# RWKV recurrence: the chunks of a head tile in turn, with norm, gate and output projection by pairs of head tiles inside the loop

## The chip, the cores and the metric

One NeuronCore of a Trainium2 chip runs the whole program. The metric is the time of one execution on the device, in microseconds (us). Engines are named as in the profile: PE is TensorE (matmuls; PEld its weight loads), DVE is VectorE, ACT is ScalarE, POOL is GpSimd, SP is SyncE, whose queue issues the transfers.

## The reference

A block of one hybrid layer (an RG-LRU beside attention, then a mixture of experts) is followed by four layers of FFN, mixer, FFN on 256 tokens of 1024 channels, batch 1, all in fp32. The mixers of layers 0 and 3 are RWKV-7 with 16 heads of 64; layer 1 is Mamba-2, layer 2 sliding-window attention. What the change touches is the end of the RWKV mixer:

```python
def step(state, inp):
    r_t, w_t, k_t, v_t, kk_t, a_t = inp
    sa = jnp.einsum('bhvk,bhk->bhv', state, -kk_t)
    state = (state * w_t[:, :, None, :] + sa[..., None] * (kk_t * a_t)[:, :, None, :]
             + v_t[..., None] * k_t[:, :, None, :])
    return state, jnp.einsum('bhvk,bhk->bhv', state, r_t)
...
mean = jnp.mean(y, axis=-1, keepdims=True)
var = jnp.mean(jnp.square(y - mean), axis=-1, keepdims=True)
y = ((y - mean) * lax.rsqrt(var + RW_GN_EPS)).reshape(bsz, seq, d) * ln_w + ln_b
bonus = jnp.sum(rh * kh * r_k, axis=-1, keepdims=True) * vh
out = ((y + bonus.reshape(bsz, seq, d)) * g).astype(h.dtype) @ w_o
...
x = x + gate[:, 1, None] * y
```

Layer 3 also mixes its values with those of layer 0 (`v_first`).

## The kernel before

Channels lie on the 128 partitions, in J = 8 tiles of 128 (two heads each); tokens lie along the free axis, T = 256 of them. The residual stream `x` is [128, 8, 256].

**Projections.** A weight slab is 1 MB, [128, 2048], loaded by SP into one of 4 buffers (tag `raw`). `slab` (lines 315 to 331) splits it in two halves of 1024 columns: ScalarE rounds a half to `hi`, VectorE takes `lo` = raw - hi; there are 3 buffers of each. `mm3` multiplies hi by the activations' hi and lo parts and lo by their hi part: three matmuls of 128x128 weights and 256 columns. `proj` runs slab after slab of 256 output channels over all eight tiles of input channels, and calls back with the sum in PSUM. `proj_parts` is the same with a stop after each quarter.

**PSUM.** Eight banks under three tags: `y` has four, `h` two, `m` two (`bank`, lines 306 to 308). The products of a step (`pk`, two banks) are in `y`; `pw`, `pa`, the turned keys, the gate's products `pg` and half of the joins are in `h`; `py`, `pS`, the broadcasts `hb` and the other joins are in `m`.

**The recurrence** (`rwkv`, lines 650 to 1080) goes by two chunks of 128 tokens. A step is one chunk c of one head tile m, and the 16 steps go through chunk 0 of all tiles and then chunk 1 of all:

```python
steps = [(c, m) for c in range(2) for m in range(J)]
```

A step has four parts, each on TensorE with a copy behind it: `products` (keys against receptances and rates, masked by VectorE, two steps ahead), `weighted` (pw, copied to ws, two steps ahead), `solve` (pa = inverse times ws, copied to sa, one step ahead) and `finish` (py, copied to Y; for chunk 0 also the state S0, which chunk 1 of the same tile reads). The inverses of I - M come from 32x32 blocks by `join(g)`, four stages for eight blocks of `Mab`; two joins of small matmuls serve chunk 0 (block index 16 c + 2 m + e) and two chunk 1. Stages of the joins and quarters of the values' projections are handed out step by step. From step 5 on, `gated` puts one tile of the gate's products through ScalarE into G. In chunk 1, v is multiplied by the bonus sums and `squares` adds up the squares of Y, four tiles to a bank.

After the loop, `normal(0)` and `normal(1)` do the group norm of four tiles each: a chain of ten small VectorE operations (`rsqrt`, lines 445 to 463), a broadcast `hb`, three VectorE operations (lines 1017 to 1019) and a split. Then the output projection runs, four slabs over all of `oh`, `ol`:

```python
normal(0, *o)
normal(1, *o)
gate, nxt = now.gate(), follow()
...
self.proj("rw", 16 * j + 12, 4, on_o, uh=o[0], ul=o[1])
```

Its callback adds gate times the sum to x (`residual`, line 515) and lets the next FFN take the tile: `Follow.tile` squares it and splits A x (lines 503, 218, 219).

**Order.** Instructions are written in program order, but a planner puts each engine's queue in order by when it reckons operands and buffers to be free, earlier text first. A queue is then served strictly in that order. Chunks of the modulation vectors (`pump`: four passes of line 422 on VectorE and two loads) are put in at steps 1, 3, 5 and 7.

Of the kernel before, what the change touches and what calls it, by code (L numbers as in the profile page):

```python
# [10 lines left out]
F32 = mybir.dt.float32  # L11
F32R = mybir.dt.float32r
# [41 lines left out]
def shape_consts():  # L54
    """Masks, selectors and the like: they depend on shapes alone."""
# [33 lines left out]
def col_list(g):  # L89
    """Vectors as columns: 128 channels on the partitions, one column per 128."""  # L90
# [39 lines left out]
# query heads whose key heads sit on the same partitions, two to a tile  # L130
# [3 lines left out]
def prepare(g):  # L134
    """The inputs as the program reads them: moved, joined and padded, nothing computed."""
    g = {k: np.asarray(v) for k, v in g.items()}
    a = {}
# [24 lines left out]
    for j in range(2):  # L162
        rw += [kxm(g["rw_w_rkv_2"][j, i]) for i in (1, 0, 2)] + [kxm(g["rw_w_o_2"][j])]
# [31 lines left out]
# ---------------------------------------------------------------- the program  # L195
class Follow:
    """What a layer's part reads of x, taken as each tile of x is done: the squares, and A x, split,
    with the shift in a column of its own. W (A x r + shift) = r W (A x) + W shift, so the products
    with A x run before r, the reciprocal norm of a token, is known."""
# [45 lines left out]
    def scaled(self, h, t):  # L245
        """t = r times the product; the product with the shift comes as a column"""
# [7 lines left out]
class Store:  # L254
    """What follows the last part: x goes out, its last two tiles on their own"""
# [10 lines left out]
class Program:  # L266
# [42 lines left out]
    # ---- weights  # L309
# [5 lines left out]
    def slab(self, name, i, n=2):  # L315
        """The slab split in two, by halves: w(o) gives the hi and lo of columns o to o + 128."""
# [34 lines left out]
    def split(self, m, t, uh=None, ul=None):  # L351
        """t [128, 256] -> uh[m] + ul[m]"""
# [4 lines left out]
    def proj(self, name, base, n, cb, kt=J, uh=None, ul=None, pump=0):  # L357
        """Slabs of columns against the split activations: cb(slab, psum [128, tiles, 256])."""
# [7 lines left out]
    def proj_parts(self, name, i, cb, kt=J, uh=None, ul=None, tag="h"):  # L366
        """One slab, and a stop after each quarter"""
# [12 lines left out]
    # ---- modulation vectors  # L380
# [6 lines left out]
    def gemv(self, name, chunk, lhs, bias, out):  # L387
        """out [128, 4] = the chunk's 512 columns of lhs @ W + bias"""
# [19 lines left out]
    def silu_rows(self, name, cb):  # L408
        """cb [128, 1024] = silu of the vector, on every partition"""
# [5 lines left out]
    def gemv_v(self, name, chunk, bias, out):  # L415
        """The same on the vector engine, from a slab of rows: [128 columns, 2, 1024]"""
# [9 lines left out]
    def pump(self, n, on_vector=False):  # L426
        """The next n chunks of those for that engine"""
# [27 lines left out]
        # with h = v (8 / 3 y) ** 2: y = y (h - 10 / 3) h + 5 y, then Newton's step  # L455
# [9 lines left out]
    def ordered(self):  # L465
        """The vector engine's work traced inside stays behind the last that was marked"""
# [5 lines left out]
    def sum_d(self, st, src, first, last):  # L472
        """st [128 t, 2] += sum of src [128, 256] over its partitions"""
# [3 lines left out]
    def bcast_t(self, r):  # L477
        """r [128 t, 2] -> [128, 256], the same on every partition"""
# [5 lines left out]
    def head_stat(self, st, m, src):  # L484
        """st [128 t, 2, n] gets the sums of src [128, 256] over 64 partitions each"""
# [3 lines left out]
    def head_bcast(self, r, m, tag="m"):  # L489
        """r [128 t, 2, n] -> [128, 256]: heads 2m and 2m + 1, 64 partitions each"""  # L490
# [22 lines left out]
    def residual(self, m, y, gate, follow=None):  # L513
        """x[m] += gate * y"""
# [5 lines left out]
    def mod2(self, i, s):  # L520
        """A and shift columns of layer i's part s"""
# [17 lines left out]
    def modulate(self, src, bc, A, sh, dst=None, follow=None):  # L539
        """src * A * bc + sh, split, or into dst's last 256 columns"""  # L540
# [13 lines left out]
    def centred(self, xc, between=None):  # L554
        """xc = x - mean over the channels; the reciprocal deviation, on every partition"""
# [16 lines left out]
    def token_major(self, w, h):  # L572
        """h [128 t, 2, 256] = the split activations times a slab of 256 columns"""
# [9 lines left out]
    # ---- FFN  # L583
# [65 lines left out]
    # ---- RWKV-7  # L649
    def rwkv(self, l, now, follow):  # L650
# [4 lines left out]
        with ExitStack() as ctx:  # L655
# [24 lines left out]
            # decay and in-context rate: h W + dx (mu W)  # L680
# [18 lines left out]
            # keys  # L699
# [44 lines left out]
            # decay from the middle of the first chunk to the middle of the second  # L744
# [10 lines left out]
            # receptance; the keys against the rates  # L755
# [13 lines left out]
            def against(m):  # L769
# [13 lines left out]
                for e in range(2):  # L783
                    for c in range(2):
                        o = 16 * c + 2 * (m - 1) + e
                        tt(Mab[:, o:o + 3:2, :], pb[e][:, c], self.k("mtri")[:, None, 0:P].to_broadcast([P, 2, P]),
# [1085 lines left out]
```

## Time and profile before

| | us |
|---|---|
| median of 3 runs | 3163.48 |
| lowest and highest | 3135.44, 3188.22 |
| span of the profiled execution | 3161.7 |
| PE busy in that span | 2998.0 (95%) |
| DVE busy | 2312.4 (73%) |
| ACT busy | 1573.8 (50%) |

The span runs from the first to the last instruction of one execution; that execution's own time is not listed apart from the three runs, and the median lies 1.8 us above the span. Busy is the time in which at least one instruction of the engine ran; a matmul's end is modelled, so a busy PE is not one at its peak. Each row of the trace gives an instruction or a group with its line in the kernel, its engine, its operation, and what it writes and reads (out<-in). The granted clock is that of TensorE: 1.00 is 2.4 GHz and 0.50 is 1.2 GHz.

### The profile page before, as it was taken

What the parts mean: (1) busy time and instruction counts of PE and PEld (TensorE: products, weight loads), DVE (VectorE), ACT (ScalarE), POOL (GpSimd) and SP (SyncE); (2) the same over time, 40 slices, a digit from 0 to 9 for tenths busy, and PEclk for the clock granted to TensorE, in tenths of its full rate; (3) what the DMA queues carried; (4) which work ended last, traced back from release to release, by engine and by line L of the source; (5) the groups of instructions that cost most, each with busy time, mean ns of one, the idle gap of its engine ahead of it and who ended that gap; (6) DMA issues with size and microseconds to landing.
All of it is one profiled execution on the core that took longest, in us unless ns stands there. A gap on an engine that the chain in (4) does not pass through costs nothing.

```text
span 3161.7 us, 56639 instructions
## 1 busy us (share of the span) xinstructions
PE 2998.0 (95%) x22903; PEld 2764.3 (87%) x22903; DVE 2312.4 (73%) x4018; ACT 1573.8 (50%) x2679; POOL 215.4 (7%) x264
## 2 busy tenths in 40 slices
PE   7979999799899999999899999999899999999999
PEld 6867887799768799999889999998799998787999
DVE  6668889676884387687788776877677776984754
ACT  5537776443522154544776545444644544432543
POOL 1200000001500000000000000000300001500000
PEclk8979999799886699999999999999899999997999
DMA  7468887585223078586354685773287583232353
GB/s 302 168 257 328 320 322 289 211 308 202 94 107 107 27 272 302 196 337 254 134 204 157 260 306 220 288 299 136 109 308 290 218 305 138 100 108 94 135 186 134
DMA packets 94757, 674.33 MB, mean 213 GB/s; under 512 B 10711, under 2 KB 12056, under 8 KB 14104
## 3 DMA queue, kind: packets, MB, share of 16 engines
q1 hardware_dynamic: 94488, 670.63, 56.8%
q8 instruction: 182, 2.98, 0.4%
q14 instruction: 87, 0.71, 0.1%
HBM read 666.87 MB, written 3.72 MB: 212 GB/s over the span
## 4 chain that ended last, share of the span: by engine, by line
PE 70%; DVE 7%; ACT 3%; issue 1%; POOL 1%; DVEq 0%; POOLq 0%; ACTq 0%
PE h L334 38%; PE y L334 15%; PE ea L334 3%; DVE lo L324 2%; PE py L334 2%; PE pk L334 1%; PE zg L334 1%; PE hb L334 1%; PE pw L334 1%; PE pg L334 1%; PE st L334 1%; PE pa L334 1%; ACT hi L323 1%; DVE ut L544 1%; PE z L334 1%
## 5 line engine op out<-in xcount | busy, mean ns | idle before, releaser
L324 DVE TENSOR_TENSOR lo<-raw,hi 128x1024 fp32r<-128x1024 f32 x897 | 1088.7, 1229 | 379.0 <-ACT hi L323 376.0
L323 ACT CAST hi<-raw 128x1024 fp32r<-128x1024 f32 x897 | 930.0, 1051 | 674.9 <-PE h L334 283.5
L334 PE MATMUL h<-uh,hi 128*128 128x256 f32 x3488 | 1000.2, 287 | 20.3 <-ACT hi L323 13.6
L334 PE MATMUL h<-uh,lo 128*128 128x256 f32 x3488 | 998.0, 286 | 15.5 <-DVE lo L324 15.5
L334 PE MATMUL h<-ul,hi 128*128 128x256 f32 x3488 | 995.9, 286 | 0.0
L334 PEld LDWEIGHTS h<-uh,hi 128*128 128x128 f32 x3488 | 669.6, 192 | 29.1 <-ACT hi L323 16.2
L334 PEld LDWEIGHTS h<-uh,lo 128*128 128x128 f32 x3488 | 669.0, 192 | 23.4 <-DVE lo L324 18.5
L334 PEld LDWEIGHTS h<-ul,hi 128*128 128x128 f32 x3488 | 669.3, 192 | 2.4 <-issue 1.7
L422 DVE SCALAR_TENSOR_TENSOR raw<-raw,cb 128x1024 f32<-128x1024 f32 x312 | 374.7, 1223 | 36.3 <-DMA raw<-in_ada 35.8
L334 PE MATMUL y<-gh,lo 128*128 128x256 f32 x1408 | 393.4, 279 | 0.0
L334 PE MATMUL y<-gh,hi 128*128 128x256 f32 x1408 | 393.4, 279 | 0.0
L334 PE MATMUL y<-gl,hi 128*128 128x256 f32 x1408 | 392.9, 279 | 0.0
L334 PEld LDWEIGHTS y<-gl,hi 128*128 128x128 f32 x1408 | 264.9, 188 | 0.0
L334 PEld LDWEIGHTS y<-gh,hi 128*128 128x128 f32 x1408 | 264.8, 188 | 0.0
L334 PEld LDWEIGHTS y<-gh,lo 128*128 128x128 f32 x1408 | 264.6, 188 | 0.0
L507 POOL TENSOR_TENSOR sq<-sq 128x256 f32<-128x256 f32 x60 | 52.8, 880 | 2239.9 <-ACT sq L503 1802.2
L354 ACT CAST gh<-g 128x256 fp32r<-128x256 f32 x176 | 71.3, 406 | 149.0 <-DVE g L613 145.8
L611 ACT ACTIVATE sa<-h 128x256 f32<-128x256 f32 x160 | 60.9, 381 | 135.0 <-PE h L334 134.5
L334 PE MATMUL eh<-hi,gh 128*128 128x512 f32 x256 | 105.2, 411 | 0.7 <-ACT hi L323 0.7
L334 PE MATMUL eh<-lo,gh 128*128 128x512 f32 x256 | 104.2, 407 | 1.7 <-DVE lo L324 1.7
L334 PE MATMUL eh<-hi,gl 128*128 128x512 f32 x256 | 102.2, 399 | 0.0
L334 PE MATMUL ea<-uh,hi 128*128 128x258 f32 x312 | 91.6, 302 | 2.0 <-ACT uh L218 2.0
(472 smaller groups left out, 4434.7 us busy)
## 6 DMA issues: line engine op xcount, KB each, us to landing
raw<-in_ffn_in SPq DMA_DIRECT2D x176, 1024.0 KB, 5.4
raw<-in_ada SPq DMA_DIRECT2D x168, 1024.0 KB, 4.9
raw<-in_w SPq DMA_DIRECT2D x96, 1024.0 KB, 4.9
raw<-in_ffn_out SPq DMA_DIRECT2D x88, 1024.0 KB, 6.6
raw<-in_rw SPq DMA_DIRECT2D x32, 1024.0 KB, 4.8
raw<-in_mb_in SPq DMA_DIRECT2D x24, 1024.0 KB, 5.0
raw<-in_w_in SPq DMA_DIRECT2D x10, 1024.0 KB, 4.9
raw<-in_mb_out SPq DMA_DIRECT2D x8, 1024.0 KB, 4.8
```

The lines of the kernel that those rows point to most:

```text
L323: self.nc.scalar.copy(hi, r[:, c])
L324: self.nc.vector.tensor_tensor(lo, r[:, c], hi.bitcast(F32), op=OP.subtract)
L334: self.pe = self.nc.tensor.matmul(out, lhs, rhs, start=start, stop=stop, skip_group_check=True)
L354: self.nc.scalar.copy(uh[:, m, :], t)
L422: nc.vector.scalar_tensor_tensor(w, w, 1.0, self.cb, op0=OP.mult, op1=OP.mult, accum_out=out[:, 2 * h + j:2 * h + j + 1])
L507: self.nc.gpsimd.tensor_tensor(self.acc, self.acc, sq, op=OP.add)
L544: self.last = nc.vector.scalar_tensor_tensor(t, src[:, m, :], A[:, m:m + 1], bc, op0=OP.mult, op1=OP.mult)
L611: nc.scalar.activation(sa, a, AF.Silu, bias=bias)
```

## The change

The two chunks of a tile go in turn, chunk 1 of a tile one tile behind chunk 0, and the blocks of `Mab` are ordered by tile, so that a join serves both chunks of two tiles. The norm, the gate and the output projection go by pairs of tiles: after chunk 1 of an odd tile, `normal` does the pair, with the gate's products read by VectorE straight from PSUM, and `project` takes the pair's 256 input channels through all of the output channels, a quarter (two output tiles) to a step, and adds each quarter to x. The output weights are laid out for that. The last pair is projected after the loop, with the FFN's `follow` opened just ahead of it. In layer 0 the values are stored by slab, as they come. Comments and docstrings are gone from the file, too.

```diff
-        rw += [kxm(g["rw_w_rkv_2"][j, i]) for i in (1, 0, 2)] + [kxm(g["rw_w_o_2"][j])]
+        rw += [kxm(g["rw_w_rkv_2"][j, i]) for i in (1, 0, 2)]
+        rw.append(g["rw_w_o_2"][j].reshape(4, 2, P, 1024).transpose(0, 2, 1, 3).reshape(4, P, 2048))
...
-                        o = 16 * c + 2 * (m - 1) + e
-                        tt(Mab[:, o:o + 3:2, :], pb[e][:, c], ...
+                        o = 4 * (m - 1) + 2 * c + e
+                        tt(Mab[:, o:o + 5:4, :], pb[e][:, c], ...
...
+                else:
+                    o = 2 * T * s
+                    nc.sync.dma_start(self.vf[:, o:o + 2 * T], v[:, 2 * s:2 * s + 2, :].rearrange("p m t -> p (m t)"))
...
-            def gated(m):
...
-            def squares(m):
...
+            o = []
+
+            def normal(i):
+                ms = (2 * i, 2 * i + 1)
+                st = self.bank([P, 2, 4], "yst", "m")
+                for m in ms:
+                    sq = self.t1("sq")
+                    act(sq, Y[:, m, :], AF.Square)
+                    self.head_stat(st, m % 2, sq)
+                ry = self.rsqrt(st.rearrange("p c n -> p (c n)"), 1.0 / 64, 64e-5, 8)
                 ry = ry.rearrange("p (c n) -> p c n", c=2)
+                if i == 0:
+                    self.new_u()
+                c = slice(2 * i, 2 * i + 2)
+                o.append((self.uh[:, c], self.ul[:, c]) if i < 3 else (self.t2("oh", F32R), self.t2("ol", F32R)))
+                for m in ms:
+                    hb = self.head_bcast(ry, m % 2)
+                    pg = self.bank([P, T], "pg", "h")
+                    self.mm(pg, L2[:, P * m:P * m + P], sg1[:, 0], True, False)
+                    self.mm(pg, L2[0:32, 1024 + P * m:1024 + P * m + P], sg1[0:32, 1], False, True)
                     t = self.t1("yo")
                     stt(t, Y[:, m, :], C("ln_w", m), hb, op0=OP.mult, op1=OP.mult)
                     stt(t, t, C("ln_b", m), v[:, m, :], op0=OP.add, op1=OP.add)
-                    tt(t, t, G[:, m, :], op=OP.mult)
-                    self.split(m, t, oh, ol)
+                    tt(t, t, pg, op=OP.mult)
+                    self.split(m % 2, t, *o[i])
+
+            def project(i, gate, nxt=None):
+                w = self.slab("rw", 16 * j + 12 + i)
+                for q in range(4):
+                    h = self.bank([P, 2, T], "h")
+                    for m in (2 * q, 2 * q + 1):
+                        for kk in range(2):
+                            self.mm3(h[:, m % 2, :], w(kk * 1024 + m * P), o[i][0][:, kk, :], o[i][1][:, kk, :],
+                                     m % 2 + kk == 0, kk == 1)
+                    for m in (2 * q, 2 * q + 1):
+                        self.residual(m, h[:, m % 2, :], gate, nxt)
+                    yield
+
+            steps = [(0, 0)]
+            for m in range(1, J):
+                steps += [(0, m), (1, m - 1)]
+            steps.append((1, J - 1))
...
-                if joins and n % 2:
+                if n == 2:
                     next(joins.pop(0))
...
                 if n == 4:
                     L2 = self.load("lora", 3 * j + 2)
-                    G = self.up.tile([P, J, T], F32, name="G", tag="uh")
-                if 5 <= n < 5 + J:
-                    gated(n - 5)
+                    gate = now.gate()
                 if c:
                     tt(v[:, m, :], v[:, m, :], self.head_bcast(bon, m), op=OP.mult)
-                    squares(m)
...
+                    if m % 2:
+                        normal(m // 2)
+                        outs += [project(m // 2, gate)] * 4 if m < J - 1 else []
+                if outs:
+                    next(outs.pop(0))
+            for part in outs:
+                next(part)
+            nxt = follow()
+            for _ in project(3, gate, nxt):
+                pass
             return nxt
```

## Rows read from the trace of the kernel before

**Rows 1.** The page: engines' busy us, granted clock in 40 slices, chain's shares.
```profile
PE 2998.0 (95%) x22903; PEld 2764.3 (87%) x22903; DVE 2312.4 (73%) x4018; ACT 1573.8 (50%) x2679; POOL 215.4 (7%) x264
...
PEclk8979999799886699999999999999899999997999
...
PE 70%; DVE 7%; ACT 3%; issue 1%; POOL 1%; DVEq 0%; POOLq 0%; ACTq 0%
```

**Rows 2.** By stretch, layer 0: us; busy of PE, PEld, DVE, ACT, POOL; clock, DMA.
```profile
927.60:961.70 34.10, 28.56 (x284) 24.44 (x284) 17.56 (x29) 9.32 (x23) 2.40 (x3) 0.50 0.35 116
961.70:989.00 27.30, 27.30 (x353) 23.42 (x352) 19.13 (x40) 9.81 (x28) 3.02 (x4) 1.00 0.61 216
989.00:1088.00 99.00, 99.00 (x523) 74.94 (x515) 20.39 (x50) 18.01 (x57) 1.46 (x2) 0.50 0.08 29
1088.00:1123.00 35.00, 32.25 (x278) 29.77 (x279) 31.38 (x67) 17.07 (x33) 5.47 (x5) 1.00 0.30 101
```

**Rows 3.** The same, layer 3.
```profile
2808.00:2866.30 58.30, 57.99 (x734) 48.74 (x730) 40.60 (x85) 24.12 (x66) 6.91 (x8) 0.94 0.45 164
2866.30:2907.30 41.00, 41.00 (x227) 30.66 (x224) 13.34 (x25) 9.11 (x24) 0.72 (x1) 0.50 0.22 78
2907.30:2935.00 27.70, 27.70 (x247) 21.61 (x248) 8.77 (x26) 8.16 (x27) 0.00 (x0) 1.00 0.12 39
2935.00:2973.00 38.00, 35.24 (x305) 32.75 (x304) 33.88 (x75) 19.07 (x35) 5.47 (x5) 1.00 0.22 80
```

**Rows 4.** Timeline of ACT: start us, us; Y copies of successive steps, layers 0, 3.
```profile
1056.61 0.27 ACT L987 COPY Y<-py 128x128 f32<-128x128 f32 x1 [1.51 <-PE py L334]
...
1066.29 0.27 ACT L987 COPY Y<-py 128x128 f32<-128x128 f32 x1 [1.51 <-PE py L334]
...
2917.19 0.27 ACT L987 COPY Y<-py 128x128 f32<-128x128 f32 x1 [0.74 <-PE py L334]
...
2922.49 0.27 ACT L987 COPY Y<-py 128x128 f32<-128x128 f32 x1 [0.74 <-PE py L334]
```

**Rows 5.** By stretch, the FFN behind layer 0's recurrence.
```profile
1139.20:1142.60 3.40, 3.40 (x19) 3.40 (x18) 3.40 (x6) 2.90 (x5) 0.00 (x0) 0.50 0.63 229
1142.60:1160.00 17.40, 17.40 (x148) 17.40 (x148) 15.06 (x20) 8.51 (x13) 0.00 (x0) 1.00 0.83 314
```

**Rows 6.** Timeline of PE, layer 3's tail: a pair's broadcasts, first and tenth projection matmul.
```profile
2935.93 1.09 PE L334 MATMUL hb<-kc,rsy 128*64 128x128 f32 x16 [0.24 <-DVE yo L1017]
...
2938.75 0.28 PE L334 MATMUL h<-oh,lo 128*128 128x256 f32 x1
...
2939.81 0.28 PE L334 MATMUL h<-oh,lo 128*128 128x256 f32 x1
```

**Rows 7.** Timeline of PE, two parts of a second-chunk step of layer 3.
```profile
2912.36 1.22 PE L334 MATMUL pg<-sg,raw 128*128 128x256 f32 x4
...
2914.63 0.70 PE L334 MATMUL pk<-AR,ka 64*128 64x256 f32 x4
```

**Rows 8.** Groups by line, 1088 to 1123 us: count, busy us, mean ns, idle before.
```profile
L324 DVE TENSOR_TENSOR lo<-raw,hi 128x1024 fp32r<-128x1024 f32 x8 | 10.2, 1284 | 0.1
...
L219 DVE SCALAR_TENSOR_TENSOR ul<-x,A,uh 128x256 fp32r<-128x256 f32 x8 | 5.4, 721 | 0.0
...
L1017 DVE SCALAR_TENSOR_TENSOR yo<-Y,cols,hb 128x256 f32<-128x256 f32 x8 | 3.7, 477 | 1.1 <-PE hb L334 1.1
L515 DVE SCALAR_TENSOR_TENSOR x<-h,mod,x 128x256 f32<-128x256 f32 x8 | 3.4, 476 | 0.9 <-PE h L334 0.9
...
L1019 DVE TENSOR_TENSOR yo<-yo,G 128x256 f32<-128x256 f32 x8 | 3.3, 420 | 0.0
...
L452 DVE TENSOR_SCALAR rsv<-yst 128x16 f32<-128x16 f32 x1 | 0.2, 175 | 1.0 <-PE yst L334 1.0
```

**Rows 9.** Timeline of SP, layer 0.
```profile
977.22 0.42 SPq L1051 DMA_DIRECT2D vf_dram<-v  x1
979.20 12.81 SPq L312 DMA_DIRECT2D raw<-in_rw  x3
```

More of the change, by code (lines that the diff above doesn't have):

```diff
@@ L784, in against @@
                     for c in range(2):
-                        o = 16 * c + 2 * (m - 1) + e
-                        tt(Mab[:, o:o + 3:2, :], pb[e][:, c], self.k("mtri")[:, None, 0:P].to_broadcast([P, 2, P]),
+                        o = 4 * (m - 1) + 2 * c + e
+                        tt(Mab[:, o:o + 5:4, :], pb[e][:, c], self.k("mtri")[:, None, 0:P].to_broadcast([P, 2, P]),
                            op=OP.mult)
@@ L827, in rwkv @@
             vz = None
+            if not l:
+                self.vf = self.dram.tile([P, J * T], F32, name="vf_dram")
             for m in range(J):
@@ L962, in solve @@
                 for e in range(2):
-                    self.mm(pa[:, e, :], Mab[:, 16 * c + 2 * m + e, :], ws[:, e, :], e == 0, True)
+                    self.mm(pa[:, e, :], Mab[:, 4 * m + 2 * c + e, :], ws[:, e, :], e == 0, True)
                 sa = self.t1("sa2").rearrange("p (h v) -> p h v", h=4)[:, 0:2]
@@ L995, in finish @@
                         nc.vector.tensor_scalar(S0[rr[e], m, rr[e]], pS[rr[e]], emid[rr[e], m:m + 1], None, op0=OP.mult)
-            def gated(m):
-                pg = self.bank([P, T], "pg", "h")
-                self.mm(pg, L2[:, P * m:P * m + P], sg1[:, 0], True, False)
-                self.mm(pg, L2[0:32, 1024 + P * m:1024 + P * m + P], sg1[0:32, 1], False, True)
-                nc.scalar.copy(G[:, m, :], pg)
-            def squares(m):
-                if m % 4 == 0:
-                    stats.append(self.bank([P, 2, 8], "yst"))
-                sq = self.t1("sq")
-                act(sq, Y[:, m, :], AF.Square)
-                self.head_stat(stats[-1], m % 4, sq)
-            def normal(g, oh, ol):
-                ry = self.rsqrt(stats[g].rearrange("p c n -> p (c n)"), 1.0 / 64, 64e-5, 16)
-                ry = ry.rearrange("p (c n) -> p c n", c=2)
-                for m in range(4 * g, 4 * g + 4):
-                    hb = self.head_bcast(ry, m % 4)
+            o = []
[7 more added lines that the diff above has]
+                ry = self.rsqrt(st.rearrange("p c n -> p (c n)"), 1.0 / 64, 64e-5, 8)
+                ry = ry.rearrange("p (c n) -> p c n", c=2)
+                if i == 0:
[7 more added lines that the diff above has]
+                    self.mm(pg, L2[0:32, 1024 + P * m:1024 + P * m + P], sg1[0:32, 1], False, True)
                     t = self.t1("yo")
@@ L1018, in normal @@
                     stt(t, t, C("ln_b", m), v[:, m, :], op0=OP.add, op1=OP.add)
-                    tt(t, t, G[:, m, :], op=OP.mult)
-                    self.split(m, t, oh, ol)
-            steps = [(c, m) for c in range(2) for m in range(J)]
-            stats = []
+                    tt(t, t, pg, op=OP.mult)
[15 more added lines that the diff above has]
+            steps.append((1, J - 1))
             joins = [st for g in range(4) for st in [join(g)] * 4]
@@ L1048, in rwkv @@
                     next(values.pop(0))
-                    if self.vf is None and not values:
-                        self.vf = self.dram.tile([P, J * T], F32, name="vf_dram")
-                        nc.sync.dma_start(self.vf, v.rearrange("p m t -> p (m t)"))
                 if n < 15:
@@ L1063, in rwkv @@
                     L2 = self.load("lora", 3 * j + 2)
-                    G = self.up.tile([P, J, T], F32, name="G", tag="uh")
-                if 5 <= n < 5 + J:
-                    gated(n - 5)
+                    gate = now.gate()
                 if c:
                     tt(v[:, m, :], v[:, m, :], self.head_bcast(bon, m), op=OP.mult)
-                    squares(m)
-            o = arr("oh", [P, J, T], "S0", F32R), arr("ol", [P, J, T], "AR", F32R)
-            normal(0, *o)
-            normal(1, *o)
-            gate, nxt = now.gate(), follow()
-            def on_o(s, h):
-                for i in range(2):
-                    self.residual(2 * s + i, h[:, i, :], gate, nxt)
-            self.proj("rw", 16 * j + 12, 4, on_o, uh=o[0], ul=o[1])
+                    if m % 2:
[8 more added lines that the diff above has]
+                pass
             return nxt
```

1 line of the change is left out of this document (added).

## The prediction

> **What bounds the kernel now.** I read the page first, then tables by stretch of the two RWKV layers (layer 0 near 740 to 1123 us, layer 3 near 2630 to 2973 us), then single steps of the recurrence. On the page TensorE is busy for 95% of the span and carries 70% of the chain that ended last; no other engine carries more than 7% [rows 1]. So a part on another engine is worth nothing unless TensorE waits for it, and TensorE's own matmuls are worth their time at the clock they get. The clock row shows where that is not full speed: the lowest pair of slices, 6 and 6, is layer 0's recurrence [rows 1].
>
> The table by stretch puts edges to it. In layer 0 the clock is at half (1.2 GHz) for 34.1 us when the joins begin, full for 27.3 us, and at half again from 989.0 to 1088.0, 99.0 us in one piece, with TensorE counted busy for all of it [rows 2]. Layer 3 has the same code and loses 41.0 us at half, then does its last steps at full [rows 3]. A second-chunk step lasts 9.68 us at half and 5.30 us at full [rows 4]: the same instructions, one behind the other on TensorE. The reader is to see that the step is bound by TensorE, and that one us at half is worth (9.68 - 5.30) / 9.68 = 0.45 us. The two long pieces cost (99.0 + 41.0) x 0.45 = 63 us, the early one 15 us more.
>
> What did TensorE do before the clock moved? In layer 0 it rose within the last step, before the first output projection matmul (the projection is in the next row, all at full); in layer 3 it rose among second-chunk steps [rows 2, 3]. So the steps alone can release it, and can also fail to for 99 us. In the FFN behind layer 0 it stood at half for 3.4 us and rose, with TensorE and its weight loads both busy for all of it: the dense products of a projection [rows 5]. In the 99 us the weight loads are busy for only 74.9 [rows 2]. Dense products are what the recurrence lacks from 989 us on, and what the change puts there.
>
> **The change, part by part.** The profiled execution's span is 3161.7 us; its own time is not listed apart from the three runs, so I add the 1.8 us between this span and their median, 3163.5.
>
> (a) Output projection in quarters inside the loop. The matmuls stay 192 a layer. They start 1.06 / 9 = 0.118 us apart [rows 6], so a quarter of 12 takes 1.4 us at full, a slab 5.7 us. Three of four slabs move into the loop. Moving them is worth nothing as work, since TensorE does them either way. What they may buy is the clock. I take that it still falls where it falls now, since the joins and the waits of the first steps stay; that the first quarter comes a norm's chain (about 8 us, below) later; and that the clock is up about 3.4 us behind it, as in [rows 5]. That leaves 11 us at half in each layer. With joins now spread over steps 3 to 10, I add a second, short fall in layer 0: 18 us there, 12 in layer 3. Gain: (99 - 18) x 0.4525 = 36.7 us and (41 - 12) x 0.4525 = 13.1 us, together **49.8 us**. Bounds: 63 us (nothing left at half) and 0. I stand nearer the first because [rows 5] is the nearest row to dense products arriving at half clock; 0 is what [rows 2] would say, since 99 us of busy matmuls released nothing.
>
> (b) Both chunks of a tile in turn. Products, corrections, broadcasts and joins are the same in number; the index of Mab, the joins' order and the weight layout cost nothing in instructions. The state of tile m is written in step 2m - 1 and read at the end of step 2m, so a step covers it; only the last tile's is read at once, which a projection quarter covers. Zero, hidden by TensorE's other matmuls; if uncovered, about a us a layer.
>
> (c) The gate's products pg no longer go through ScalarE to G: 8 copies a layer fewer. ScalarE is busy for 18.0 us of the 99 [rows 2], so 0, and 0 without that cover too, since it is work taken away. But the bank of pg is now held until VectorE's third operation of the norm. The tag h has two banks, and pa, pw, the turned keys and half of the joins need them. A pair's chain from the squares' sums: ten small operations of 0.175 us, the broadcast 1.09, two of 0.477 and one of 0.420 [rows 6, 8], 4.2 us until the first bank is free, 1.4 us more for the second. Behind it stand the next step's pa, and ScalarE, which turns pa into sa. TensorE can do pk for the step after next (0.70 us and its third part) and a quarter (1.4 us), and pg itself takes 1.22 us [rows 6, 7]: some 3.5 us of cover. Bounds: 0 (the planner brings pg late) and 4.2 us for each of six pairs, 25 us. I take 1.5 us a pair, nearer to the covered end: **+9 us**.
>
> (d) VectorE: 24 more residual additions of 0.476 us and two more chains of ten a layer, 15 us [rows 8]. In the 99 us stretch it is busy for 20.4 us [rows 2], so 0; without that cover, 15 us a layer. Splitting the slabs (1.28 us each half on VectorE) does not change in number.
>
> (e) Queues. The stored first values go out in 4 transfers instead of one, of 0.42 us of issue [rows 9]. The four weight slabs are loaded by SP as before, and the planner already asks for them from 979 us, long before the loop's end [rows 9]; their split halves take turns in the same buffers, and a slab's two halves now go free together, after its last quarter, so the next is split in the step between. The multiplication of v by the bonus must wait for that read, but each part leaves steps before. Zero. The gate vector is asked for at step 4, with its modulation chunks already taken by earlier pumps: zero; one chunk more there would be four passes on VectorE in its idle time.
>
> (f) The tail. Now normalisation and projection of different tiles overlap, and TensorE idles 2.75 us in each tail [rows 2, 3]. After it, the last pair's chain (norm 4.2, second tile 1.4, square, copy and split about 2, so 8 us) is covered by its own broadcasts, pg and one quarter, about 5 us. Then 5.7 us of matmuls face 8 x (0.476 + 0.72) = 9.6 us of residuals and splits of x, and slab splits between [rows 8]. The FFN's first products take the tiles as they come. I take 2 us more a layer, **+4 us**; bounds 0 and 12 for both.
>
> Sum: 3161.7 - 49.8 + 9 + 4 = 3124.9, with the 1.8 us **3127 us**, 1.2% below the median.
>
> **The rivals.** Rival 1, the clock does not move: a quarter of 1.4 us in a step is too thin, or the planner, which orders the queues by its own readiness, lets the quarters slip behind the loop. For it: 99 us at half with a busy engine [rows 2]. Against: every long row with projections in it is at full [rows 2, 3]. Then only the costs stay: 3163.5 + 9 + 4 = 3176. The Trainium skill (TensorE: Matmul & The Clock Gate, section Part 1: The HAM clock gate) says that half rate is the default and that recent busyness of TensorE releases it. Read with the page's busy time, that rule would leave the clock alone, as the engine is busy all along already, and give this rival's time. The trace does not agree with it in that form, 99.00 us busy at half.
>
> Rival 2, slower: the two h banks. If the planner brings pg ahead of the norm's chain, both are held 5.6 us a pair and no pa, pw or turned keys run; TensorE stands, and the clock's gain is not had. 8 x 5.6 = 45 us: 3208. It decides against the change as soon as the clock stays; with the clock's gain it needs over 49.8 / 8 = 6.2 us a pair. For it: two banks, and [rows 8]'s chain. Against: the products of the step after next use other banks.
>
> Rival 3, the whole clock: also the early 34.1 us go, 174.1 x 0.4525 = 78.8 us, with +4: 3089. For it: layer 3's joins begin without such a piece, at 0.94 over 58.3 us [rows 3]. Against: that fall lies ahead of the first changed step.
>
> **How the numbers follow.** Forecast 62%, its own range 3100 (63 us gained, no costs) to 3157 (half of 63 gained, 25 us of waits); rival 1 14%, rival 2 10%, rival 3 14%. The range 3086 to 3172 leaves out rival 2 and the upper half of rival 1. By over 2% (63 us, about what a measurement can tell from no change here, the three runs lying 53 us apart) faster means below 3100: rival 3 and the edge of the forecast, 20%; slower, above 3227: the far end of rival 2, 4%; within 76%.
>
> **What would show it.** Steps: a table by stretch of layer 0 with less than 30 us at half from the first quarter on, and second-chunk steps without the 9.68 us beat. (c): TensorE's idle time ahead of pa, released by VectorE's product with pg. (f): idle time in the stretch from the last Y copy to the FFN's first products, above 2.75 us. The prediction is wrong if the half-clock total of the two layers stays above 110 us, or if it falls and the time does not.

## The result: 0.7% slower, and the profile after

Over 20 runs of each the kernel after takes 3176.4 us in the median (3161.8 to 3203.0), the kernel before 3159.9 (3131.1 to 3191.3); the ratio is 1.0073, 95% interval [1.0046, 1.0101]. Forecast were 3127 us and a gain of 1.2%. The profiled execution has a span of 3174.2 us. The medians of the table below leave out executions over 1.5% above the fastest of their kernel: one of e3_order, one of e16_guard and three of the six of e8_split_late.

The page of the kernel after: busy us of the engines, the granted clock in 40 slices, the chain's shares.

```profile
PE 2990.2 (94%) x22903; PEld 2764.5 (87%) x22903; DVE 2338.9 (74%) x4106; ACT 1567.7 (49%) x2663; POOL 216.5 (7%) x264
...
PEclk8979999899988799999999999998999999988899
...
PE 68%; DVE 9%; ACT 3%; issue 1%; POOL 1%; DMA 0%; DVEq 0%; POOLq 0%; ACTq 0%; SPq 0%
```

Beside [rows 1] the low pair of slices in layer 0 is better (8 and 7 for 6 and 6); at layer 3, three slices running show an 8 where one showed a 7. VectorE has taken 2% of the chain from TensorE.

The kernel after by stretch: layer 0 from the first products to the last Y copy and from there to the FFN's first activation, then the same of layer 3 (us; busy of PE, PEld, DVE, ACT, POOL; clock; DMA).

```profile
902.40:1098.10 195.70, 177.74 (x1467) 149.88 (x1466) 106.76 (x225) 47.22 (x119) 8.73 (x10) 0.74 0.24 87
1098.10:1132.90 34.80, 31.49 (x254) 29.16 (x251) 31.09 (x74) 24.85 (x48) 4.07 (x5) 1.00 0.65 242
2772.50:2957.90 185.40, 162.84 (x1455) 137.44 (x1456) 108.33 (x234) 48.33 (x125) 10.53 (x10) 0.81 0.24 91
2957.90:2995.10 37.20, 33.91 (x235) 31.23 (x232) 30.44 (x74) 22.46 (x46) 3.94 (x5) 0.86 0.29 114
```

The same two loops in the kernel before:

```profile
904.60:1086.30 181.70, 174.51 (x1295) 140.33 (x1296) 78.39 (x155) 44.08 (x117) 7.04 (x10) 0.64 0.24 88
2788.70:2933.60 144.90, 140.25 (x1287) 113.07 (x1288) 80.64 (x164) 44.87 (x123) 7.90 (x10) 0.84 0.31 109
```

The reader is to see two things. The piece of 99 us at half [rows 2] is gone: the clock of layer 0's loop is 0.74 in the mean for 0.64, that of layer 3's 0.81 for 0.84. And TensorE is idle for 18.0 us of layer 0's loop and 22.6 of layer 3's, where it was for 7.2 and 4.7. The waits name why.

The waits of TensorE in the kernel after, layer 0 from 990 us, then layer 3 from 2845 us: who waited for whom, us in total, times, longest.

```profile
PE hb L335 <- DVE rsy L463: 8.6, 3, 3.6
...
PE pa L335 <- DVE yo L1027: 1.0, 1, 1.0
PE px L335 <- DVE yo L1027: 0.9, 1, 0.9
```

```profile
PE hb L335 <- DVE rsy L463: 14.0, 3, 8.9
PE px L335 <- DVE yo L1027: 2.1, 2, 1.2
...
PE pa L335 <- DVE yo L1027: 1.0, 1, 1.0
```

TensorE stands at the norm's broadcast hb until VectorE's ten operations (L453 to L463) are done: once a pair, six times, 22.6 us; then at px or pa for VectorE's product with pg (L1027), 5 us more. The timeline of TensorE around the first pair of layer 3 (start us, us, operation) shows how the queue stands there.

```profile
2851.11 0.66 PE L335 MATMUL hb<-kc,bon 128*64 128x128 f32 x8
2851.70 0.70 PE L335 MATMUL pg<-sg,raw 128*128 128x256 f32 x2
2852.24 0.50 PE L335 MATMUL yst<-kc,sq 128*128 128x2 f32 x4
2852.67 0.69 PE L335 MATMUL pg<-sg,raw 32*128 32x256 f32 x2
2853.29 0.61 PE L335 MATMUL yst<-kc,sq 128*128 128x2 f32 x4
2862.77 1.97 PE L335 MATMUL hb<-kc,rsy 128*64 128x128 f32 x16 [8.87 <-DVE rsy L463]
2864.55 0.69 PE L335 MATMUL py<-mkr,vtok 128*64 128x128 f32 x4
2865.03 0.64 PE L335 MATMUL py<-mkr,sa 128*64 128x128 f32 x4
2866.87 1.44 PE L335 MATMUL px<-T,Mab 64*64 64x64 f32 x11 [1.20 <-DVE yo L1027]
```

Both tiles' pg are done ahead of the chain and hold both h banks. What needs an h bank (px, pa) can't stand next, and hb is put ahead of the py that needs none. VectorE in that wait, a few of its rows:

```profile
2853.94 0.17 DVE L453 TENSOR_SCALAR rsv<-yst 128x8 f32<-128x8 f32 x1 [1.70 <-PE yst L335]
2854.02 1.22 DVE L423 SCALAR_TENSOR_TENSOR raw<-raw,cb 128x1024 f32<-128x1024 f32 x1
...
2856.91 0.16 DVE L455 TENSOR_SCALAR rsy<-rst 128x8 int32<-128x8 int32 x1
2856.98 1.21 DVE L423 SCALAR_TENSOR_TENSOR raw<-raw,cb 128x1024 f32<-128x1024 f32 x1
...
2862.46 0.17 DVE L463 SCALAR_TENSOR_TENSOR rsy<-rst,rsy 128x8 f32<-128x8 f32 x1
```

Passes of 1.2 us stand between the chain's operations, which is why this wait is 8.87 us and those of the later pairs 2.55. What the waits do to the clock shows in a table of six stretches of layer 3: steps, wait, steps, twice over.

```profile
2875.00:2898.70 23.70, 23.68 (x274) 19.64 (x272) 11.55 (x23) 7.49 (x21) 0.73 (x1) 1.00 0.14 46
2898.70:2901.60 2.90, 0.36 (x6) 0.36 (x8) 2.15 (x10) 0.00 (x0) 0.72 (x1) 1.00 0.00 0
2901.60:2915.20 13.60, 12.75 (x68) 9.76 (x64) 5.07 (x12) 2.29 (x6) 0.00 (x0) 0.50 0.00 0
2915.20:2936.40 21.20, 21.19 (x192) 17.65 (x190) 10.50 (x21) 5.94 (x17) 0.73 (x1) 1.00 0.14 51
2936.40:2939.20 2.80, 0.25 (x5) 0.21 (x6) 2.15 (x10) 0.00 (x0) 0.72 (x1) 1.00 0.00 0
2939.20:2949.40 10.20, 9.24 (x49) 7.29 (x45) 4.37 (x11) 1.24 (x4) 0.00 (x0) 0.50 0.00 0
```

Full clock, a wait of 2.55 us, then half clock for 13.6 and for 10.2 us. So there are two suspects for the loss: the waits by their length, and the clock that they seem to take with them.

### The profile page after: what moved, and what is told of

Its sections match the earlier page's. It is cut to its first block, busy times and chain, and to the rows that moved or that the text cites. A ratio compares the mean times of both kernels' runs of the same rounds, so it can differ in the third digit from the quotient of the medians.

```text
span 3174.2 us, 56689 instructions
## 1 busy us (share of the span) xinstructions
PE 2990.2 (94%) x22903; PEld 2764.5 (87%) x22903; DVE 2338.9 (74%) x4106; ACT 1567.7 (49%) x2663; POOL 216.5 (7%) x264
## 4 chain that ended last, share of the span: by engine, by line
PE 68%; DVE 9%; ACT 3%; issue 1%; POOL 1%; DMA 0%; DVEq 0%; POOLq 0%; ACTq 0%; SPq 0%
PE h L335 39%; PE y L335 15%; PE ea L335 3%; DVE lo L325 2%; PE pk L335 1%; PE py L335 1%; PE hb L335 1%; PE st L335 1%; ACT hi L324 1%; PE pw L335 1%; PE pa L335 1%; PE zg L335 1%; DVE ut L545 1%; PE pg L335 1%; PE px L335 1%
## 5 line engine op out<-in xcount | busy, mean ns | idle before, releaser
L335 PE MATMUL h<-uh,hi 128*128 128x256 f32 x3584 | 1035.8, 289 | 19.2 <-ACT hi L324 13.3
L335 PE MATMUL h<-uh,lo 128*128 128x256 f32 x3584 | 1031.7, 288 | 12.3 <-DVE lo L325 12.3
L335 PE MATMUL h<-ul,hi 128*128 128x256 f32 x3584 | 1031.2, 288 | 0.0
L335 PEld LDWEIGHTS h<-uh,hi 128*128 128x128 f32 x3584 | 694.2, 194 | 29.5 <-ACT hi L324 16.0
L335 PEld LDWEIGHTS h<-uh,lo 128*128 128x128 f32 x3584 | 693.1, 194 | 20.9 <-DVE lo L325 14.9
L335 PEld LDWEIGHTS h<-ul,hi 128*128 128x128 f32 x3584 | 694.1, 194 | 7.9 <-DVE ul L356 3.7
L508 POOL TENSOR_TENSOR sq<-sq 128x256 f32<-128x256 f32 x60 | 49.8, 830 | 2109.6 <-ACT sq L504 1640.0
L335 PE MATMUL ea<-uh,lo 128*128 128x258 f32 x312 | 90.5, 295 | 0.9 <-DVE lo L325 0.9
```

The source lines that it names most:

```text
L335: self.pe = self.nc.tensor.matmul(out, lhs, rhs, start=start, stop=stop, skip_group_check=True)
L508: self.nc.gpsimd.tensor_tensor(self.acc, self.acc, sq, op=OP.add)
```

## The experiments

**How they are read.** Each run lists its span and mean granted clock. Half-clock us are 2 x (1 - clock) x span, over the whole program; with the 0.4525 us that one of them costs [rows 4], a run's time is split into clock and rest (span less 0.4525 x half-clock). Over the 20 runs of the kernel after, time against half-clock has a slope of 0.43; over those of the other kernels with nine runs or more it lies between 0.33 and 0.49. So where two kernels differ by 80 us at half, the split is uncertain by some 10 us. Each kernel was run beside the kernel before, and the ratio is to those runs; the row of before is of the 35 runs beside e1 to e5. Its half-clock was the same beside e6 to e15, and 411 us (median 3165.5) beside e16 and e17. Medians over the runs, us:

| kernel | ratio to before, 95% | median | half-clock | rest |
|---|---|---|---|---|
| before | | 3160 | 398 | 2978 |
| after | 1.0073 [1.0046, 1.0101] | 3176.4 | 387 | 2999 |
| e1_copy | 0.9977 [0.9949, 1.0004] | 3150.7 | 340 | 2995 |
| e3_order | 1.0035 [1.0000, 1.0070] | 3164.2 | 399 | 2981 |
| e4_oldorder | 1.0021 [0.9993, 1.0048] | 3161.2 | 373 | 2991 |
| e5_split | 0.9937 [0.9914, 0.9960] | 3139.5 | 342 | 2985 |
| e6_split_copy | 0.9929 [0.9901, 0.9958] | 3128.8 | 316 | 2983 |
| e7_pumps | 1.0073 [1.0043, 1.0103] | 3177.0 | 390 | 2997 |
| e8_split_late | 1.0133 [1.0077, 1.0190] | 3172.2 | 399 | 2990 |
| e9_split_copy_pumps | 0.9953 [0.9926, 0.9980] | 3140.9 | 345 | 2984 |
| e10_copy_late | 1.0112 [1.0089, 1.0134] | 3199.5 | 470 | 2985 |
| e11_chain | 1.0096 [1.0081, 1.0110] | 3190.6 | 389 | 3013 |
| e12_split_chain | 0.9994 [0.9982, 1.0005] | 3156.3 | 372 | 2985 |
| e13_split2_copy | 0.9947 [0.9930, 0.9964] | 3145.0 | 352 | 2986 |
| e14_stall24 | 0.9957 [0.9920, 0.9993] | 3142.1 | 336 | 2988 |
| e15_stall8 | 0.9953 [0.9914, 0.9992] | 3135.5 | 329 | 2985 |
| e16_guard | 1.0096 [1.0057, 1.0136] | 3188.2 | 421 | 2999 |
| e17_guard_free | 0.9912 [0.9884, 0.9941] | 3132.9 | 319 | 2984 |

The kernel after gained 11 us at half, worth 5, and lost 21 us in the rest: 16 us, as measured.

**e1_copy: the held banks.**

```diff
+                    gm = self.t1("gm")
+                    nc.scalar.copy(gm, pg)
...
-                    tt(t, t, pg, op=OP.mult)
+                    tt(t, t, gm, op=OP.mult)
```

> The kernel after, but ScalarE copies the gate's product pg out of its h bank at once, as the kernel before did, so the bank is free without VectorE's norm (16 copies more, all of the computation kept). Theory 1 (the norm's broadcast hb heads TensorE's queue and waits for VectorE's ten-operation chain: 8.6 us in layer 0, 14.0 in layer 3): those waits stay, the waits of pa and px for the product with pg (5 us in both layers) go; ratio to the kernel before 1.004 to 1.008, about 3172 us. Theory 2 (the held banks are the cost, step (c) of the prediction, up to rival 2): most of what was lost comes back, ratio 1.000 or below, 3160 us or less.

Theory 2's result: the loss is gone. But not as expected of it: the rest fell by 4 us only, less than the split can tell, and half-clock by 47. With the banks free px and pa stand ahead of hb. The waits of hb come to 1.6 and 7.4 us in layers 0 and 3 for 8.6 and 14.0, and the first pair's wait in layer 3 is 5.87 instead of 8.87 us:

```profile
2831.32 0.61 PE L335 MATMUL yst<-kc,sq 128*128 128x2 f32 x4
2831.85 1.14 PE L335 MATMUL px<-T,Mab 64*64 64x64 f32 x16
2833.66 0.66 PE L335 MATMUL pa<-ws,Mab 128*128 128x64 f32 x4 [0.67 <-ACT xs L942]
2840.19 1.98 PE L335 MATMUL hb<-kc,rsy 128*64 128x128 f32 x16 [5.87 <-DVE rsy L463]
```

So theories 1 and 2 are one: the held banks leave hb at the head of the queue.

**e3_order: the order alone.** The steps list, the index of Mab, the joins' and the stores' edit of the change, put into the kernel before.

> The kernel before with the order alone: both chunks of a tile in turn, the index of Mab, the joins' order and the stores of the first values as in the kernel after; norm, gate's copies and projection as before, behind the loop. Theory 1: the order costs nothing, ratio 0.998 to 1.002, half-clock pieces of layer 0 about as long as before (100 to 130 us in all). Theory 4 (the order itself costs: joins bunched in the first ten steps, the state of a tile read sooner): ratio 1.004 to 1.010 here, with waits of TensorE for VectorE or ScalarE among the steps.

Rest +3, half-clock +1: the interval reaches from nothing to 0.7%. No wait above 0.5 us was added among the steps. That alone does not exclude theory 4, but e5 and e6 below keep the order and are faster than the kernel before, so it is not needed.

**e4_oldorder: the pairs in the old order.** The same lines, but for the stores', undone in the kernel after.

> The kernel after with the order of before: first chunk of all tiles, then the second, joins and Mab's index as before; norm, gate and projection by pairs inside the loop, now at steps 9, 11, 13 and 15, all behind the modulation passes of steps 1 to 7. Theory 1 (chain ahead of hb on TensorE, whatever else VectorE does): four waits of about 3 us a layer, 24 us in both, less what the quarters give to the clock: ratio 1.000 to 1.006. Theory 3 (the chain is late because the modulation passes of 1.2 us stand between its ten operations): waits of hb under 2 us each, and the clock's gain shows: ratio 0.985 to 0.995.

With the passes over before the first pair, the page of waits has none of hb left, as theory 3 has it. The ratio is theory 1's: half-clock is 25 us below that of the kernel before, and the rest 13 above. TensorE's idle time over the whole page is that of before (163.8 us for 163.7), so no wait says by what. Part may be the split's own error; the rest stays open.

**e5_split: hb one step behind its chain.**

```diff
-                        normal(m // 2)
-                        outs += [project(m // 2, gate)] * 4 if m < J - 1 else []
+                        due.append((n + 1, m // 2, normal(m // 2)))
+                if due and n in (due[0][0], 15):
+                    _, i, ry = due.pop(0)
+                    apply(i, ry)
+                    outs += [project(i, gate)] * 4 if i < 3 else []
```

> The kernel after with the norm in two parts: squares, sums and the ten-operation chain of a pair at its step, the broadcast hb, pg, the product and the projection's first quarter one step later (for the last pair at once, behind the loop). Theory 1: the waits of hb shrink from 22.6 us to under 8, TensorE is idle under 15 us in layer 3's stretch instead of 25.9, and the time falls below the kernel before: ratio 0.990 to 1.000. If the waits shrink and the time does not, the clock takes it back (rival 1); if the waits stay, a step is too short for the chain (theory 3).

As theory 1 has it: of the waits of hb one of 3.4 us is left, the rest is 14 us below that of the kernel after and half-clock 45 us. It beats both kernels.

**e6_split_copy, e9_split_copy_pumps, e13_split2_copy: both cures, and more of them.** e6 is e5 with e1's edit; e9 moves the passes on top, e13 puts two steps for one.

> The norm in two parts a step apart (as in e5_split) and the gate's product copied out of its bank by ScalarE (as in e1_copy), both in one. If the two costs are different ones (hb at the head of TensorE's queue; held banks) their gains add: against the kernel after, the split gave 1.35% and the copy 0.95%, so the ratio to the kernel before would be about 0.984. If they are one cost seen from two sides (the held banks leave the planner nothing but hb to put next), the second gives nothing more: 0.992 to 0.996.

> e6_split_copy with the modulation passes at steps 0 to 3. If theory 3 holds beside the others: the last wait of hb (3.4 us in layer 3 of e5_split) goes too, and the ratio is 0.001 to 0.003 below that of e6_split_copy. If not: the same as e6_split_copy within 0.002.

> e6_split_copy with two steps between a pair's chain and its hb instead of one. If one step covers the chain already: the same time, 0.991 to 0.995, less whatever later quarters lose on the clock; if the first pair's chain in layer 3 is still late among the modulation passes (3.4 us of wait in e5_split): 0.002 lower.

e6 is at 0.9929, not 0.984: one cost seen from two sides. In its profile TensorE has no wait above 1.0 us behind the first joins (px, 4.7 and 4.4 us, and between 4.3 and 5.2 us in every other kernel). e9 and e13 have the same rest and 29 and 36 us more at half-clock; their intervals meet that of e6. Nothing to gain there. e6, and e17 below at 0.9912, are the fastest versions; e5, e9, e13, e14 and e15 have intervals below 1, too.

**e7_pumps: the passes.** `"rwkv": (1, 3, 5, 7)` becomes `(0, 1, 2, 3)`.

> The kernel after with the modulation passes put in at steps 0, 1, 2 and 3 instead of 1, 3, 5 and 7, so that all sixteen are traced ahead of the first pair's norm; nothing else. Theory 3 (the first pair's chain is late because passes of 1.2 us stand between its operations): the 8.9 us wait of hb in layer 3 falls under 4, ratio 1.002 to 1.005 to the kernel before. Theory 1 or 2 alone: the wait stays, or the joins' own work on VectorE moves into its place, ratio 1.006 to 1.009.

The wait of 8.9 us went down to 4.6, and the time did not move: 1.0073, as for the kernel after, with an interval of 9 us to either side. Theory 3 explains the length of that wait; what its 4.3 us are worth is too little for these runs to show, and the loss is still there without them.

**e8_split_late and e10_copy_late: the quarters, step (a) by itself.** In e5_split and in e6_split_copy:

```diff
-                if outs:
-                    next(outs.pop(0))
             for part in outs:
                 next(part)
```

> e5_split with the projection of all pairs behind the loop: the norm stays inside by pairs in two parts, no quarter runs among the steps. What the prediction's step (a) claims for the quarters is then tested by itself. If the quarters hold the clock up: half-clock in layer 0 back from 89 to 110 us or more, in layer 3 from 51 to 70 or more, ratio 1.000 to 1.008. If they do nothing for the clock and only fill waits: half-clock as in e5_split, ratio 0.993 to 0.998.

> e6_split_copy (no wait of hb or for the banks left) with the projection of all four pairs behind the loop. It asks again, in the undisturbed kernel and against e6_split_copy on its own, what the quarters among the steps are worth: step (a) priced them at 49.8 us, all of it clock. If step (a) is right: half-clock over the whole program 80 to 110 us above that of e6_split_copy (316 us median of its runs), ratio to the kernel before 1.004 to 1.010. If the clock came back through the missing waits alone: half-clock within 25 us of e6_split_copy, ratio 0.992 to 0.998.

e10 against e6: half-clock 470 for 316, rest 2985 for 2983, so 70 us, all of it clock, more than was expected. The six executions of e10 stand at 439 to 481 us at half, the twelve of e6 at 274 to 352. e8 against e5 points the same way (399 for 342), but decides little: its six executions stand at 314 to 502, and its ratio does not agree with the medians, which give 1.0036. Its profile, of the fastest of the six, has 89 and 26 us at half in layers 0 and 3, where 110 and 70 were expected. The loops of e10 by stretch (layers 0 and 3), then those of e6:

```profile
903.40:1094.20 190.80, 182.94 (x1333) 144.99 (x1332) 90.03 (x198) 45.20 (x122) 6.92 (x10) 0.64 0.22 78
...
2786.50:2968.20 181.70, 175.41 (x1323) 140.41 (x1322) 91.71 (x208) 46.41 (x127) 8.63 (x10) 0.67 0.22 81
```

```profile
903.30:1067.70 164.40, 155.90 (x1453) 128.41 (x1454) 102.57 (x222) 48.77 (x125) 7.49 (x10) 0.85 0.30 103
...
2739.70:2898.60 158.90, 151.58 (x1445) 126.47 (x1444) 104.27 (x232) 50.06 (x131) 7.75 (x10) 0.88 0.30 106
```

Some 120 matmuls more in e6's loop, in 23 to 26 us less. TensorE is idle for 6 to 9 us in each: in e10, as in [rows 2], a busy engine without quarters stays at half for long. In this kernel the quarters hold the clock up.

**e11_chain and e12_split_chain: a longer chain.** Ten operations more between the chain and hb, in the kernel after and in e6:

```diff
+                for _ in range(10):
+                    nc.vector.tensor_scalar(ry, ry, 1.0, None, op0=OP.mult)
```

> The kernel after with ten more multiplications by one on the 128x8 result of each pair's chain: no value changes, the chain from the squares' sums to hb is about twice as long (1.75 us more a pair, 14 us over eight pairs, by 0.175 us an operation). Theory 1 (hb heads TensorE's queue, so the chain's time is TensorE's): the waits of hb grow by 10 to 14 us over both layers, and the time by that and something more for the clock: ratio 1.011 to 1.018 to the kernel before. If the chain is hidden and the loss lies elsewhere: 1.007, as the kernel after.

> The same ten operations a pair in e6_split_copy, where hb comes a step later. Theory 1: a step covers the longer chain, only the last pair of a layer shows it (3.5 us in both): ratio 0.992 to 0.995 against 0.993 for e6_split_copy. If VectorE's time itself were the cost, both kernels would lose alike: 0.997 or more.

In e11 (four runs) the waits of hb come to 17.3 and 23.7 us, 18 more than in the kernel after, four a layer for three. The rest rises by 14 us, half-clock not at all (389 for 387), and the ratio stays just below the range. The chain's time is TensorE's time, and a longer wait takes no more clock than a short one. In e12 the rest is e6's within 2 us, as expected, but 56 us more at half cost 25: waits of hb of 3.9 us in each tail and 4.7 in layer 3 are there again. The expected time was missed.

**e14_stall24 and e15_stall8: waits put back, first try.**

```diff
+                    for _ in range(24 if n in (5, 9, 13) else 0):
+                        nc.scalar.copy(sa[n + 1], sa[n + 1])
```

> e6_split_copy with 24 copies of sa onto itself on ScalarE (0.266 us each, 6.4 us) at steps 5, 9 and 13 of each layer, ahead of the py that reads it: no value changes, TensorE has to wait at the same three places of a layer as in the kernel after, but for ScalarE and not for the norm's chain. If a wait of TensorE by itself drops the clock: waits of 2 to 5 us at six places (12 to 30 us), a fall of the clock behind most of them, half-clock 50 us or more above the 316 us of e6_split_copy, ratio 1.008 to 1.018 to the kernel before. If the wait costs only itself: half-clock within 25 us of e6_split_copy, ratio 0.997 to 1.003.

> The same with 8 copies (2.1 us), which the products, the quarter and pg that stand ahead of py in TensorE's queue should cover: waits under 1 us each, half-clock and time as in e6_split_copy, ratio 0.991 to 0.996. If it is ScalarE's work as such, or the shifted order of the queue, that costs: 0.997 or more.

Inconclusive. Other matmuls were put ahead of the py that waits for sa; behind the joins e14's waits are 2.4 us in one loop, and 2.0 in each tail. Half-clock rose by 20 us, with intervals that meet.

**e16_guard and e17_guard_free: waits put back, second try.** In e6_split_copy, behind each of the first three chains; e17 reads a constant where e16 reads ry:

```diff
+                    self.mm(gd[0:64, 0:P], ry[:, 0, 0:1].to_broadcast([P, 64]), self.k("ident"))
+                    guard.append(self.pe)
...
+                if guard:
+                    hold.enter_context(self.tc.issue_after(guard.pop().ins))
```

> e6_split_copy with one extra 64x128 matmul (gd, its product read by no one) behind each chain of the first three pairs, reading the chain's result, and all of TensorE's work traced in the next step kept behind it in the queue. So TensorE waits for the chain at the same six places as in the kernel after, while the banks are free and hb still comes a step later. If a wait drops the clock: waits of 15 to 30 us in all, a fall of the clock right behind each, half-clock 45 us or more above e17_guard_free, ratio 1.006 to 1.015 to the kernel before. If a wait costs only itself: half-clock within 25 us of e17_guard_free, ratio 0.998 to 1.003.

> e16_guard with the extra matmul reading a constant instead of the chain's result: the same instruction, the same forced order of the queue, no wait. Both theories: the time of e6_split_copy, ratio 0.991 to 0.997. If the forced order itself costs (the quarter and the products can no longer change places across the step): above 0.998, and e16_guard is to be read against this kernel, not against e6_split_copy.

This tells them apart: 1.0096 against 0.9912, with intervals far from each other. The waits of e16, layer 0 and layer 3:

```profile
PE gd L335 <- DVE rsy L463: 10.5, 3, 3.7
```

```profile
PE gd L335 <- DVE rsy L463: 15.1, 3, 7.7
```

25.6 us of waits at six places cost 61 us by the table (55.3 between the medians): 15 in the rest, and 46 for 102 us more at half-clock. The executions of e16 stand at 374 to 476 us at half, those of e17 at 280 to 359. e16 in two stretches around the second wait of layer 3, then the steps behind it; and e17's steps from the hb of its first pair on:

```profile
2866.00:2890.00 24.00, 24.00 (x276) 19.35 (x274) 12.02 (x27) 6.43 (x22) 1.46 (x2) 1.00 0.01 1
2890.00:2896.00 6.00, 2.33 (x19) 2.11 (x18) 4.37 (x14) 1.99 (x2) 0.00 (x0) 0.76 0.12 16
2896.00:2927.20 31.20, 31.20 (x156) 23.72 (x154) 8.13 (x18) 4.17 (x13) 0.72 (x1) 0.50 0.07 31
```

```profile
2821.20:2831.40 10.20, 9.75 (x60) 7.87 (x60) 7.56 (x18) 2.05 (x4) 2.70 (x1) 0.50 0.65 252
2831.40:2914.00 82.60, 80.71 (x742) 66.23 (x742) 52.48 (x135) 30.38 (x82) 6.09 (x8) 1.00 0.18 69
```

One wait of 3.67 us and the clock is at half for 31 us of busy steps. In e17 it falls once among these steps, for 10.2 us, at a wait of 1.51 us of that hb for its chain, which was not meant to be there; without waits the remaining steps run at full to the end. No bank, no hb and no modulation pass has a part in e16's wait.

Not all that these two profiles differ by lies behind the waits, though. Up to the first of the six both have 181 us at half; from there on e16 has 130 us more. Of these, 79 lie behind the waits, 14 in the layers between and in the tails, and 38 in layer 3 ahead of its first added wait. There a wait that both have (px for VectorE, L873, 4.35 us) is followed by 41 us at half in e16, and by 3.4 in e17:

```profile
2783.90:2824.80 40.90, 40.06 (x332) 35.01 (x334) 20.16 (x39) 14.03 (x32) 3.43 (x3) 0.50 0.29 100
```

```profile
2763.20:2766.60 3.40, 3.40 (x18) 3.18 (x16) 3.06 (x6) 1.87 (x4) 0.09 (x1) 0.50 0.15 29
```

So the waits cost what the runs say, but that all of the clock's share falls right behind them is not shown.

## Why the prediction was wrong

**Step (c) failed, and took step (a) with it.** Step (c) priced the held banks at 9 us, by 3.5 us of other work that TensorE could do meanwhile. That work was there, but hb stood ahead of it in the queue, and it started behind hb: TensorE waited 27.6 us (8.6 + 14.0 for hb, 5.0 for px and pa; e5 and e6 take most of it away). I expected the wait at pa; the longer one came earlier, at hb. Rival 2 had named the condition, pg ahead of the chain and both banks held, and that the clock's gain is then not had; the 10% on it was too little, and its 45 us for waits alone were too many.

**Step (a): the mechanism was right, its premise was not.** Quarters lift the clock: 70 us between e10 and e6. The 99 us piece broke up, and in e6, without the waits, half-clock is 82 us below that of the kernel before, a gain of 37 us where I took 49.8. But the sum assumed that the clock falls only where it fell before. It now falls at or just behind each pair's waits. In layer 3 it stays at half for 17, 14 and 10 us; layer 0's pieces are these:

```profile
993.60:1003.80 10.20, 8.47 (x54) 6.87 (x55) 4.62 (x16) 1.56 (x4) 0.00 (x0) 0.50 0.09 36
1038.00:1058.40 20.40, 20.40 (x107) 17.20 (x106) 5.48 (x13) 1.86 (x7) 0.72 (x1) 0.50 0.00 1
1072.10:1096.00 23.90, 20.94 (x110) 17.56 (x111) 8.87 (x27) 2.99 (x10) 0.31 (x1) 0.50 0.00 1
```

With one of 3.4 us more they come to 99 us in both layers. What stands at half ahead of the first pair's norm, at the joins and the first steps, grew, too: 44 and 31 us in layers 0 and 3 for 34 and 7, with no new wait above 0.5 us there, and no run shows why. In the profiles the two layers have 184 us at half where they had 181, above the 110 that the prediction named as a sign of its being wrong. 5 us of the 49.8 were left by the medians. I had set waits and clock down as two terms that add; e16 and e17 show that waits take clock with them. In e16 the clock's share, 46 us, is the larger one. A reading was off as well: in layer 0 of the kernel before the clock rose at 1088.0 us, behind the last Y copy (1086.1) and among the norm's first broadcasts; that the steps alone can release it rests on layer 3.

The Trainium skill (TensorE: Matmul & The Clock Gate, section Loop structure matters more than you think) says that matmuls kept back to back stay warm, and that a loop with a long wait for a DMA between every matmul runs cold. e16 against e17 agrees, with waits for VectorE: 421 us at half for 319. Read alone it would not have given e10, which has no wait above 1.8 us behind the joins, and 470 us at half.

**The other steps.** (b), nothing: e3 moved the rest by 3 us. (d), nothing: VectorE's additional work as such is free (after has 26.5 us more of it on the page), but its passes between the chain's operations made the longest wait 8.87 us, which I had not seen; e7, with 4.3 us of it gone, shows no measurable time for that. (e), nothing: the sixteen passes a layer are as many as before, and no wait for a queue or a slab shows among the steps. (f), 4 us more idle in the tails, did not come: it is 3.3 us in each, with 2.0 of them for the last pair's split, against 52.40 - 45.98 = 6.4 and 50.10 - 47.31 = 2.8 us in the same stretches of the profile before, 2.6 us less in all:

```profile
1086.30:1138.70 52.40, 45.98 (x388) 42.57 (x385) 45.21 (x100) 29.55 (x56) 5.47 (x5) 0.98 0.42 161
2933.60:2983.70 50.10, 47.31 (x409) 44.44 (x406) 44.86 (x100) 28.65 (x54) 5.47 (x5) 1.00 0.28 106
```

**The rivals.** Rival 1's time, 3176 us, is the measured one to the us, by luck. It stood on 3163.5 us, the median of three runs, where twenty give 3159.9, so its 13 us of costs are to be held against 16.5. And its reason is not the one that the runs show: the clock did move, up by the quarters and down with the waits. A number that fits does not show a mechanism. Rival 3 did not come: with all waits gone 316 us stay at half.

**Still open.** Why one wait takes 7 us of clock and another 34, and why the same wait ahead of the first pair takes 3.4 us in e17 and 41 in e16. And e12 and e4 have 25 us and 13 us that their waits explain only in part.

## What to carry to other kernels

In a kernel whose clock stands at half in some stretches and at full in others, price a new wait by its length and by what the clock loses behind it; here 25.6 us of waits cost 61. So put a step's distance between a chain of small operations and the matmul that reads it, and free a PSUM bank before the chain rather than behind it. Dense products are worth moving among thin ones (70 us here), but only if nothing of the move makes TensorE stand.

## What the runs showed of the hardware

- TensorE's clock falls at single waits of 2.5 to 3.7 us and stays at half for 7 to 34 us (after: 10 to 24; e16: 6.8 behind two waits of 3.67 us in layer 0, 34.1 and 23.9 behind two in layer 3). 18 us more of waits at the same places (e11, four runs) took no more.
- TensorE can be busy without a wait and stand at half for long: 85 us in one piece in layer 3 of e10.
- The first piece at half in layer 0, from the joins on, lasted 44 us in the profile of the kernel after, 17 in that of e6 and 58 in that of e12. The runs of e6 have mean clocks from 0.944 to 0.956 and times from 3116 to 3142 us. A profile of one execution does not tell two such kernels apart; medians over the runs do.
